# Low parts of weights on GpSimd instead of VectorE, and split products instead of float32 ones, in two sparse-attention layers

## The chip, the core and the metric

The kernel runs on one core of one Trainium2 chip. The metric is the device time of one execution in microseconds. The engines are named as in the profile: PE is TensorE's matmuls, PEld its weight loads, DVE is VectorE, ACT is ScalarE, POOL is GpSimd and SP is SyncE, which issues nearly all transfers.

## The reference

256 tokens of 1024 features go through two models in a row. The first is an mLSTM mixer, a convolutional feed-forward net (FFN), causal attention and a second FFN. The second model is a stack of two equal sparse-attention layers with weights of their own, and the change concerns these two alone. One of them is, in short:

```python
p = h @ w_in[l]                       # h: normalised, modulated input
u_val, u_gate, g_conv, c_q, c_kv, k_idx, w_idx, g_attn = jnp.split(p, offsets, axis=-1)
y_conv = conformer_conv(u_val, u_gate, ...) * silu(g_conv)
                                      # GLU, causal depthwise conv of 31 taps, layer norm, swish, w_pw2
y_attn = dsa_attention(c_q, c_kv, k_idx, w_idx, ...) * silu(g_attn)
                                      # scores of 8 index heads, top 64 keys per query, softmax, values
y = jnp.concatenate([y_conv, y_attn], axis=-1) @ w_out[l]
x = x + gate * rmsnorm(y, g_post[l])
```

All of it is float32, and the output has to agree to float32 accuracy.

## The kernel before, in words

**Products.** A product of two float32 operands is made in one of two ways. A *split* product writes each operand as the sum of a high part, rounded to the shorter format `float32r`, and a low part, the rest. Three matmuls are accumulated: high by high, high by low, low by high (`mm3`, lines 569 to 571). A *float32* product is one matmul instruction on the operands as they are (`mm`, line 422), which shows as two records in the trace.

**Weight pieces.** `Chunk` loads weights from HBM in pieces of up to 128 x 1024 (912 columns for `w_lat`) into a page of pool F. If it is to be split, `split_w` has ScalarE round the piece into one R page (`act`, line 435), and VectorE subtract that from the piece into a second R page (`tt`, line 448). There are 25 F pages and 24 R pages; a piece holds its buffers from the first use to the last.

**A layer.** `dsa_layer` runs once per layer. Its pieces are, in the order of the program: `w_lat` (4 pieces; queries, latent keys and values, index keys), `w_qidx` (1; index queries), `w_u` (4 chunks `u0` to `u3` of 2; gated linear unit), `w_uq` (2; queries), `w_ga` and `w_gc` (2 chunks of 2 each; gates), `w_out` rows 4 to 7 (`oa`, 4; the attention's part of the output projection), `w_pw2` (`pw`, 2; pointwise product of the convolution branch) and `w_out` rows 0 to 3 (`oc`, 4). That makes 33 pieces. The chunks named in `NATIVE`, which are `oa`, `u3`, `w_ga1` and `w_gc1` (10 pieces), are used unsplit in float32 products; the other 23 are split. The attention's four results per layer, which meet `oa`, stay unsplit for the same reason.

**Convolution.** From the four blocks `us` VectorE makes 4 x 30 fused multiply-adds (`stt`, line 453), the taps, with a mean over channels added on the way; the mean goes out to HBM (`zscr`) and back. Then come a sum of squares on PE (operand `con`), the layer norm, `pw` and `oc`.

**Order.** `Program.order` plans at build time. It goes through time with an estimated duration of each instruction, and at each step an engine takes the ready instruction that stands first in the program, if buffers for its results are free. The plan fixes each engine's order; at run time each engine works in that order and waits on semaphores. The taps have late places in the program (`CONV0`, `CONV1`), so they fill VectorE's free time, and top-k has early ones (`TOPK`).

Of the kernel before, what the change touches and what calls it, by code (L numbers as in the profile page):

```python
# [14 lines left out]
ALU = mybir.AluOpType  # L15
# [4 lines left out]
NFF = FF // 128  # L20
# [26 lines left out]
# pages of on-chip memory: name -> (columns, dtype, count)  # L47
# [6 lines left out]
# buffers: name -> (page, part of a page, columns)  # L54
# [33 lines left out]
NATIVE = {"oa", "u3", "w_ga1", "w_gc1"}  # L88
# [4 lines left out]
class Buf:  # L93
    """A slot of a pool from its first to its last use, or a tile of its own (ap given)."""
# [10 lines left out]
class V:  # L105
    """A view of a Buf: rows p0..p1, columns c0..c1, then a function of the access pattern.
    iv: the intervals of columns that it touches, where these are not all of c0..c1."""
# [33 lines left out]
class Program:  # L141
    """Records the kernel's instructions in order, then fixes the order in which each engine issues its own:
    the first in the program among those whose operands and buffers are ready."""
# [39 lines left out]
    @staticmethod  # L183
    def spread(ops, p0, p1):
        """Gives ops the priorities of the program's positions p0..p1."""
        for i, op in enumerate(ops):
            op.prio = p0 + (p1 - p0) * (i + 0.5) / len(ops)

    def order(self, slots):
        """slots: page name -> list of tiles. Returns the ops in the planned order, with table loads."""  # L190
# [30 lines left out]
        # the place for a buffer: an opened page with the least room if it is a small one, else a whole page  # L221
# [160 lines left out]
def build(ctx, tc, a):  # L382
# [57 lines left out]
    # has the activation table ready for what comes after x  # L440
# [70 lines left out]
    # the part of FIRST that begins at each of n columns, then of the next  # L511
# [7 lines left out]
    hold = [None]  # L519

    def split_w(raw, n):
        hi, lo = new("w", n), new("w", n)
        op = act(hi, raw, AF.Copy)
        if hold[0]:
            pg.after(op, hold[0])
        tt(lo, raw, hi.f32, ALU.subtract)
        return hi, lo

    class Chunk:
        """k blocks k0..k1 of a chunk of weights; split, or as it is (native) for a float32 product; cuts: in pieces."""  # L530

        def __init__(self, dram, kc, mc, k0=0, native=False, cuts=None):
            self.mc, self.kp, self.k0 = mc, 1024 // mc, k0
            self.parts = []
            for k in range(k0, kc, self.kp):
# [11 lines left out]
                self.parts.append((raw, None) if native else split_w(raw, n))  # L547
# [12 lines left out]
    # a product of split operands: high*high + high*low + low*high  # L560
# [14 lines left out]
    # two heads' values v[s][e] by their transposed probabilities p[e], each on a half of the partitions (and of the array's columns)  # L575
# [8 lines left out]
    # tokens t of x (stationary) by weights w, token-major  # L584
# [35 lines left out]
    # 1 / sqrt(ms) for a few columns, with a Newton step  # L620
# [10 lines left out]
    # sums over partitions of the squares; n blocks are added before  # L631
# [31 lines left out]
    # products of zeros while the first operands arrive, for the tensor engine's clock  # L663
# [5 lines left out]
    # ================= mLSTM mixer =================  # L669
    # The norm's factor r of a token is left out of the products here: q and the value of h do not depend on it,  # L670
    # k carries it in the exponent, v, o and the gates take it afterwards.
# [11 lines left out]
    # values of the first head, and the gates  # L683
# [134 lines left out]
    # h += w^T x  # L818
# [9 lines left out]
    # ================= conv FFN =================  # L828
# [16 lines left out]
    # quarter q of the token-major copy of h  # L845
# [7 lines left out]
    def ffn(l, h, hm=None, prep=None, head=None):  # L853
# [7 lines left out]
        # the first products start before the norm's factor is known  # L861
        def up(j):
            ps = gemm_pair(Chunk(a["f_w_up"][l * NFF + j], 8, 256), xg if j < HEAD else xs)
# [17 lines left out]
        def down(j):  # L881
            if j == 0:
                acc.extend(psum() for _ in range(4))
            ch = Chunk(a["f_w_down"][l * NFF + j], 1, 1024)
# [37 lines left out]
    # ================= shared keys/values and causal attention =================  # L922
# [19 lines left out]
    # heads' normed and rotated rows (token-major), then transposed  # L942
# [33 lines left out]
    # softmax over keys of -(neg + addm): normalised probabilities, transposed, [s, 256 | 128]  # L976
# [45 lines left out]
    # ================= second block =================  # L1022
    # sums of the four columns 4t..4t+3 into column 4t
# [5 lines left out]
    # 1 / sqrt(mean + EPS) from the parts of a sum of squares, the last of them added on the way  # L1029
# [26 lines left out]
    # the second block's part that needs only one half t of the tokens: norm (token-major), then features on partitions  # L1056
    class Head:
# [8 lines left out]
        # shift and scale of the features; the output's gain as a row  # L1066
# [46 lines left out]
    def prep():  # L1113
        ts(cwh[:, 0:248], cwh[:, 0:248], 0.5, None, ALU.mult)
        # the convolution's bias less its mean over channels
        bsum, bp = small(8), psum()
        mm(bp[:, 0:8], ones, pcols("conv_b_2", 0, 8), True, True)
        vcopy(bsum, bp[:, 0:8])
        for l in range(2):
            sums4(bsum, l)  # L1120
            ts(bcen[:, l * 4:l * 4 + 4], pcols("conv_b_2", l * 4, 4), bsum_scaled(bsum, l), None, ALU.add)
        for hd in heads:
            hd.prep()
# [3 lines left out]
    # relative position bias, as a Toeplitz band: T5[h][p, j] = -bias(128 + p - j)  # L1127
# [19 lines left out]
    def dsa_layer(l, h, last):  # L1147
        hd, xs = heads[l], heads[l].xs
        lw = Chunk(a["w_lat"][l], 8, 456)
# [3 lines left out]
        for t in range(2):  # L1153
            # latent queries, latent keys/values, index keys and weights
# [26 lines left out]
        # index queries, scores  # L1181
        hold[0] = None
        ch = Chunk(a["w_qidx"][l], 2, 512)
# [19 lines left out]
        # top 64 keys of each query  # L1203
# [13 lines left out]
        # convolution branch: gated linear unit, causal depthwise convolution  # L1217
# [3 lines left out]
        for j in range(4):  # L1221
            ps = gemm_pair(Chunk(a["w_u"][l * 4 + j], 8, 256, 0, f"u{j}" in NATIVE), xs)
# [7 lines left out]
        # its mean over channels: sums for each tap, then over taps, each row moved by its tap  # L1230
        # (a channel group's 31 taps and a row of no use on 32 partitions)
# [23 lines left out]
        # queries  # L1255
        hold[0] = None
        ch = Chunk(a["w_uq"][l], 2, 1024)
# [12 lines left out]
        def gate(i):  # L1270
            nme, j = ("w_ga", "w_gc")[i // 2], i % 2
            ps = gemm_pair(Chunk(a[nme][l * 2 + j], 8, 256, 0, f"{nme}{j}" in NATIVE), xs)
# [7 lines left out]
        # attention over the selected keys  # L1280
# [8 lines left out]
        for hp in range(4):  # L1289
# [16 lines left out]
            mix[4 + hp] = (None, None, t) if "oa" in NATIVE else split_x(t)  # L1306
        hd.load_gain()
        # layer norm over channels, swish, pointwise
# [5 lines left out]
        for j in range(4):  # L1314
# [3 lines left out]
            ln.append((None, None, t2) if "pw" in NATIVE else split_x(t2))  # L1318
        preload("E", t2)
        # output projection, attention's part  # L1320
        acc = [[(c0, c1, psum()[:, 0:c1 - c0]) for c0, c1 in zip(cuts, cuts[1:])] for cuts in OCUTS[l]]
        for k in range(4, 8):
            ch = Chunk(a["w_out_2"][l * 8 + k], 1, 1024, 0, "oa" in NATIVE)
# [3 lines left out]
        ch = Chunk(a["w_pw2"][l], 4, 512, 0, "pw" in NATIVE)  # L1327
        for j in range(2):
# [4 lines left out]
            for b in range(2):  # L1333
                t = blk()
                tt(t, half(ps, b), gates[4 + 2 * j + b], ALU.mult)
                mix[2 * j + b] = (None, None, t) if "oc" in NATIVE else split_x(t)
        chs = [Chunk(a["w_out_2"][l * 8 + k], 1, 1024, 0, "oc" in NATIVE) for k in range(4)]
# [130 lines left out]
```

## Time and profile before

| | us |
|---|---|
| three timed runs | 874.07, 874.16, 875.2 |
| median | 874.16 |
| span of the profiled execution (first to last instruction) | 873.5 |
| TensorE matmul busy | 859.4 (98%) |
| VectorE busy | 731.6 (84%) |
| ScalarE busy | 559.4 (64%) |
| GpSimd busy | 0.2 |

The profiled execution's own time is not given apart from its span; it is one of the same kernel whose runs stand 0.6 to 1.7 us above that span. The sparse-attention layers take about the last third of the span; the FFN ahead of them and they overlap in the trace, because weights are loaded and split ahead of their use. An instruction's row gives start and duration; instructions of one engine overlap a little, so the distance from start to start is what one costs its engine. Matmul ends are modelled.

### The profile page before, as it was taken

Reading aid. Unit: us, or ns where it says so; the run is one execution under the profiler, and the core shown is the slowest. Engines: PE = TensorE matmul, PEld = TensorE weight load, DVE = VectorE, ACT = ScalarE, POOL = GpSimd, SP = SyncE. Lnnn points to the kernel's source line nnn. Section 1 sums busy time; section 2 is a strip of 40 time slices with the busy share of each in tenths; the row PEclk is TensorE's granted clock in tenths of the full one; section 3 lists DMA queues with packets and bytes.
Section 4 is the critical chain, followed back from the end, with each engine's and each line's share of the span. In section 5 each row is a group of like instructions: output and inputs, shape, how many; then the busy total and the mean of one; then the engine's idle time right before and its main releaser. Section 6 shows DMA issues by size and latency. Waiting matters only on the chain.

```text
span 873.5 us, 16714 instructions
## 1 busy us (share of the span) xinstructions
PE 859.4 (98%) x6270; PEld 804.2 (92%) x6270; DVE 731.6 (84%) x1677; ACT 559.4 (64%) x1170; POOL 0.2 (0%) x4
## 2 busy tenths in 40 slices
PE   8999999999999999999999999999999999998997
PEld 8999999999999999999989999998998858997866
DVE  6757899899977699987899986675799898798895
ACT  6846577545555496874776546556953797952883
POOL 0000000000000000000000000000000000000000
PEclk9999999999999999999999999999999999999999
DMA  8987766989865354478369985642340177440101
GB/s 317 408 307 228 257 201 200 322 293 319 295 219 179 111 192 134 138 252 301 121 204 355 349 282 175 192 122 86 123 143 13 27 237 302 134 125 13 58 16 49
DMA packets 50409, 170.33 MB, mean 195 GB/s; under 512 B 5860, under 2 KB 8428, under 8 KB 50328
## 3 DMA queue, kind: packets, MB, share of 16 engines
q1 hardware_dynamic: 50184, 169.26, 56.8%
q8 instruction: 49, 0.80, 0.4%
q14 instruction: 32, 0.26, 0.1%
q10 hardware_dynamic: 144, 0.00, 0.0%
HBM read 167.88 MB, written 1.37 MB: 194 GB/s over the span
## 4 chain that ended last, share of the span: by engine, by line
PE 95%; DMA 2%; ACT 1%; DVE 1%; SPq 0%; issue 0%; DVEq 0%; ACTq 0%
PE ps L569 26%; PE ps L570 26%; PE ps L571 26%; PE ps L422 14%; PE ps L426 2%; DMA F<-zscr 1%; PE ps L580 1%; ACT F L435 1%; DMA F<-in_a_w_v_dram 1%; DVE F L453 0%; DMA zscr<-F 0%; ACT R L435 0%; DVE R L448 0%; SPq L1244 0%; PE ps L1237 0%
## 5 line engine op out<-in xcount | busy, mean ns | idle before, releaser
L569 PE MATMUL ps<-R,R 128*128 128x256 f32 (+3 forms) x1788 | 531.8, 297 | 1.3 <-ACT R L435 1.2
L570 PE MATMUL ps<-R,R 128*128 128x256 f32 (+3 forms) x1788 | 522.8, 292 | 0.5 <-DVE R L448 0.5
L571 PE MATMUL ps<-R,R 128*128 128x256 f32 (+3 forms) x1788 | 522.5, 292 | 0.0
L448 DVE TENSOR_TENSOR R<-F,R 128x1024 fp32r<-128x1024 f32 (+4 forms) x339 | 324.3, 983 | 42.0 <-ACT R L435 31.3
L569 PEld LDWEIGHTS ps<-R,R 128*128 128x128 f32 x1788 | 343.5, 192 | 10.2 <-ACT R L435 2.3
L570 PEld LDWEIGHTS ps<-R,R 128*128 128x128 f32 x1788 | 343.7, 192 | 6.8 <-DVE R L448 1.2
L571 PEld LDWEIGHTS ps<-R,R 128*128 128x128 f32 x1788 | 343.4, 192 | 5.7 <-DVE R L448 0.5
L435 ACT ACTIVATE R<-F 128x1024 fp32r<-128x1024 f32 (+4 forms) x339 | 283.1, 864 | 30.6 <-DVE F L448 24.0
L422 PE MATMUL ps<-F,F 128*128 128x256 f32 (+6 forms) x568 | 128.9, 378 | 0.9 <-ACT F L435 0.8
L435 ACT ACTIVATE F<-ps 128x256 f32<-128x256 f32 (+3 forms) x197 | 70.6, 389 | 78.3 <-PE ps L571 37.7
L422 PEld LDWEIGHTS ps<-F,F 128*128 128x128 f32 (+2 forms) x568 | 89.9, 190 | 19.6 <-issue 8.9
L435 ACT ACTIVATE F<-ps,par 128x256 f32<-128x256 f32 (+1 forms) x84 | 42.3, 552 | 93.7 <-PE ps L571 93.3
L453 DVE SCALAR_TENSOR_TENSOR F<-ps,par,F 128x255 f32<-128x255 f32 (+1 forms) x160 | 66.0, 475 | 30.7 <-ACT F L435 30.7
L453 DVE SCALAR_TENSOR_TENSOR F<-F,par,F 128x256 f32<-128x256 f32 (+11 forms) x146 | 66.5, 463 | 1.2 <-ACT F L435 1.2
L435 ACT ACTIVATE F<-F 128x256 f32<-128x256 f32 (+2 forms) x120 | 46.7, 413 | 29.7 <-DVE F L453 17.8
L453 DVE SCALAR_TENSOR_TENSOR F<-F,F 128x1024 f32<-128x1024 f32 x48 | 58.0, 1217 | 0.0
L453 DVE SCALAR_TENSOR_TENSOR F<-F,par 128x255 f32<-128x255 f32 (+14 forms) x126 | 57.8, 460 | 0.0
L448 DVE TENSOR_TENSOR F<-ps,F 128x256 f32<-128x256 f32 (+2 forms) x80 | 32.8, 439 | 21.6 <-PE ps L571 16.2
L435 ACT ACTIVATE F<-F,s 128x128 f32<-128x128 f32 (+1 forms) x80 | 33.3, 445 | 4.9 <-DVE s L474 3.8
L435 ACT ACTIVATE R<-F,par 128x256 fp32r<-128x256 f32 x32 | 14.3, 505 | 28.9 <-DVE F L448 28.9
L1364 ACT ACT_TABLE_LOAD x23 | 29.5, 1283 | 0.4
L426 PE MATMUL ps<-con,F 128*128 128x128 f32 (+2 forms) x158 | 29.4, 271 | 0.1
(96 smaller groups left out, 370.9 us busy)
## 6 DMA issues: line engine op xcount, KB each, us to landing
F<-in_f_w_up_dram SPq DMA_DIRECT2D x88, 512.0 KB, 5.3
F<-in_w_ada_dram SPq DMA_DIRECT2D x48, 512.0 KB, 5.1
F<-in_f_w_down_dram SPq DMA_DIRECT2D x44, 512.0 KB, 5.9
F<-in_w_u_dram SPq DMA_DIRECT2D x16, 512.0 KB, 5.3
F<-in_w_out_dram SPq DMA_DIRECT2D x16, 512.0 KB, 3.8
F<-in_a_w_o_dram SPq DMA_DIRECT2D x8, 512.0 KB, 10.2
F<-in_a_w_out_dram SPq DMA_DIRECT2D x8, 512.0 KB, 10.2
F<-in_w_k_dram SPq DMA_DIRECT2D x8, 512.0 KB, 5.3
```

Source lines behind the costliest of these rows:

```text
L422: pg.add("PE", dur, lambda: nc.tensor.matmul(g(out), g(lhsT), g(rhs), start=start, stop=stop, skip_group_check=not check), [lhsT, rhs], [out])
L426: pg.add("PE", 110.0, lambda: nc.tensor.transpose(g(out), g(x), g(idn)), [x, idn], [out])
L435: nc.scalar.activation(g(out), g(x), func, bias=g(bias), scale=g(scale), **kw)
L448: return pg.add("DVE", ddur(n or x.n), lambda: nc.vector.tensor_tensor(g(out), g(x), g(y), op), [x, y], [out])
L453: nc.vector.scalar_tensor_tensor(g(out), g(x), g(s), g(y), op0, op1, **kw)
L569: nc.tensor.matmul(o, g(lh), g(rh), start=start, stop=False, **kw)
L570: nc.tensor.matmul(o, g(lh), g(rl), start=False, stop=False, **kw)
L571: nc.tensor.matmul(o, g(ll), g(rh), start=False, stop=stop, **kw)
L580: nc.tensor.matmul(g(out[e * 64:e * 64 + 64, c]), g(v[s][e]), g(p[e][:, r]), start=s == 0, stop=s == 1, skip_group_check=True)
L1364: nc.scalar.preload_act_table_set(TABLE[op[1]])
```

## The change

It leaves the first model as it is. In both sparse-attention layers the low part of every weight piece is made by GpSimd instead of VectorE, and the four groups that were float32 products are split like the others, with the results that meet them. The planner books 30 + 2.4 n ns for a subtraction of n columns on GpSimd. FFN chunks now carry names too, none of which is in `BY_POOL`.

```diff
-NATIVE = {"oa", "u3", "w_ga1", "w_gc1"}
+BY_POOL = {"oa","oc","pw","uq","u0","u1","u2","u3","w_ga0","w_ga1","w_gc0","w_gc1","lat","qi"}
...
-    def split_w(raw, n):
+    def split_w(raw, n, by_pool):
         hi, lo = new("w", n), new("w", n)
         op = act(hi, raw, AF.Copy)
         if hold[0]:
             pg.after(op, hold[0])
-        tt(lo, raw, hi.f32, ALU.subtract)
+        if by_pool:
+            pg.add("POOL", 30 + 2.4 * n, lambda: nc.gpsimd.tensor_tensor(g(lo), g(raw), g(hi.f32), ALU.subtract), [raw, hi], [lo])
+        else:
+            tt(lo, raw, hi.f32, ALU.subtract)
         return hi, lo
...
                 load(raw, dram[:, k * mc:k * mc + n])
-                self.parts.append((raw, None) if native else split_w(raw, n))
+                self.parts.append(split_w(raw, n, name in BY_POOL))
...
-            mix[4 + hp] = (None, None, t) if "oa" in NATIVE else split_x(t)
+            mix[4 + hp] = split_x(t)
```

The calls of `Chunk` in `dsa_layer` pass the name instead of the membership in `NATIVE`; nothing else is changed but comments.

## Rows read from the trace of the kernel before

**Rows 1.** The page's busy times: engine, busy us, share of span, instructions.

```profile
PE 859.4 (98%) x6270; PEld 804.2 (92%) x6270; DVE 731.6 (84%) x1677; ACT 559.4 (64%) x1170; POOL 0.2 (0%) x4
```

**Rows 2.** The table by stretches: length, busy of PE, PEld, DVE, ACT, POOL; clock, DMA.

```profile
612.00:636.00 24.00, 24.00 (x171) 22.70 (x170) 18.87 (x31) 22.57 (x58) 0.00 (x0) 1.00 0.46 144
654.00:712.00 58.00, 56.58 (x346) 45.65 (x344) 54.38 (x175) 35.24 (x89) 0.00 (x0) 1.00 0.19 59
740.00:765.00 25.00, 25.00 (x170) 23.10 (x170) 18.95 (x36) 23.82 (x63) 0.00 (x0) 1.00 0.49 149
783.00:844.00 61.00, 57.95 (x360) 47.51 (x360) 55.12 (x178) 37.05 (x91) 0.00 (x0) 1.00 0.09 31
```

**Rows 3.** The same table for line 453 (fused multiply-adds) alone, the tap stretches.

```profile
654.00:712.00 58.00, 48.75 (x125) 1.00 0.19 59
783.00:844.00 61.00, 48.91 (x125) 1.00 0.09 31
```

**Rows 4.** The timeline of layer 1: start, duration, engine, line; VectorE, ScalarE, then TensorE.

```profile
843.23 0.45 DVE L453 SCALAR_TENSOR_TENSOR F<-F,par,F 128x226 f32<-128x226 f32 x1
...
848.68 0.42 ACT L435 ACTIVATE R<-F 128x256 fp32r<-128x256 f32 x1
...
850.58 0.47 PE L569 MATMUL ps<-R,R 128*128 128x256 f32 x1
```

**Rows 5.** The chain of waits, layer 0: start, duration, records of float32 products.

```profile
692.13 0.43 PE ps L422 x2
...
703.80 0.86 PE ps L422 x2
```

**Rows 6.** TensorE's timeline, first matmuls of neighbouring split products, 512 then 256 columns.

```profile
550.91 0.39 PE L569 MATMUL ps<-R,R 128*128 128x512 f32 x1
...
551.59 0.39 PE L569 MATMUL ps<-R,R 128*128 128x512 f32 x1
...
552.98 0.28 PE L569 MATMUL ps<-R,R 128*128 128x256 f32 x1
...
553.34 0.28 PE L569 MATMUL ps<-R,R 128*128 128x256 f32 x1
```

**Rows 7.** Groups by shape, 540 us to the end: count, busy us, mean ns.

```profile
L448 DVE TENSOR_TENSOR R<-F,R 128x1024 fp32r<-128x1024 f32 x55 | 66.2, 1220 | 7.6 <-ACT R L435 4.0 <-issue 3.2 <-PE ps L571 0.3
...
L435 ACT ACTIVATE R<-F 128x1024 fp32r<-128x1024 f32 x54 | 56.3, 1052 | 0.0
...
L448 DVE TENSOR_TENSOR R<-F,R 128x256 fp32r<-128x256 f32 x40 | 16.4, 422 | 11.1 <-ACT R L435 11.1
```

**Rows 8.** VectorE's timeline, subtractions of weight pieces ahead of the tap stretches, both layers.

```profile
634.67 1.23 DVE L448 TENSOR_TENSOR R<-F,R 128x1024 fp32r<-128x1024 f32 x1 [0.27 <-ACT R L435]
...
637.18 1.23 DVE L448 TENSOR_TENSOR R<-F,R 128x1024 fp32r<-128x1024 f32 x1
...
652.29 1.21 DVE L448 TENSOR_TENSOR R<-F,R 128x1024 fp32r<-128x1024 f32 x1
...
764.14 1.23 DVE L448 TENSOR_TENSOR R<-F,R 128x1024 fp32r<-128x1024 f32 x1 [0.33 <-ACT R L435]
...
766.70 1.23 DVE L448 TENSOR_TENSOR R<-F,R 128x1024 fp32r<-128x1024 f32 x1
...
781.82 1.20 DVE L448 TENSOR_TENSOR R<-F,R 128x1024 fp32r<-128x1024 f32 x1
```

**Rows 9.** VectorE's waits in 783 to 844 us: total, times, longest.

```profile
DVE F L464 <- PE ps L422: 2.6, 2, 2.4
DVE F L453 <- PE ps L422: 2.0, 1, 2.0
```

More of the change, by code (lines that the diff above doesn't have):

```diff
@@ L525, in split_w, with __init__ @@
             pg.after(op, hold[0])
-        tt(lo, raw, hi.f32, ALU.subtract)
+        if by_pool:
+            pg.add("POOL", 30 + 2.4 * n, lambda: nc.gpsimd.tensor_tensor(g(lo), g(raw), g(hi.f32), ALU.subtract), [raw, hi], [lo])
+        else:
+            tt(lo, raw, hi.f32, ALU.subtract)
         return hi, lo
     class Chunk:
-        def __init__(self, dram, kc, mc, k0=0, native=False, cuts=None):
+        def __init__(self, dram, kc, mc, k0=0, name=None, cuts=None):
             self.mc, self.kp, self.k0 = mc, 1024 // mc, k0
@@ L862, in up @@
         def up(j):
-            ps = gemm_pair(Chunk(a["f_w_up"][l * NFF + j], 8, 256), xg if j < HEAD else xs)
+            ps = gemm_pair(Chunk(a["f_w_up"][l * NFF + j], 8, 256, 0, f"up{l}{j}"), xg if j < HEAD else xs)
             if j == 0:
@@ L883, in down @@
                 acc.extend(psum() for _ in range(4))
-            ch = Chunk(a["f_w_down"][l * NFF + j], 1, 1024)
+            ch = Chunk(a["f_w_down"][l * NFF + j], 1, 1024, 0, f"down{l}{j}")
             if hm:
@@ L1148, in dsa_layer @@
         hd, xs = heads[l], heads[l].xs
-        lw = Chunk(a["w_lat"][l], 8, 456)
+        lw = Chunk(a["w_lat"][l], 8, 456, 0, "lat")
         lat = [psum() for _ in range(2)]
@@ L1182, in dsa_layer @@
         hold[0] = None
-        ch = Chunk(a["w_qidx"][l], 2, 512)
+        ch = Chunk(a["w_qidx"][l], 2, 512, 0, "qi")
         qix = []
@@ L1221, in dsa_layer @@
         for j in range(4):
-            ps = gemm_pair(Chunk(a["w_u"][l * 4 + j], 8, 256, 0, f"u{j}" in NATIVE), xs)
+            ps = gemm_pair(Chunk(a["w_u"][l * 4 + j], 8, 256, 0, f"u{j}"), xs)
             th, u2, y = blk(), blk(), blk()
@@ L1256, in dsa_layer @@
         hold[0] = None
-        ch = Chunk(a["w_uq"][l], 2, 1024)
+        ch = Chunk(a["w_uq"][l], 2, 1024, 0, "uq")
         qs = []
@@ L1271, in gate @@
             nme, j = ("w_ga", "w_gc")[i // 2], i % 2
-            ps = gemm_pair(Chunk(a[nme][l * 2 + j], 8, 256, 0, f"{nme}{j}" in NATIVE), xs)
+            ps = gemm_pair(Chunk(a[nme][l * 2 + j], 8, 256, 0, f"{nme}{j}"), xs)
             for b in range(2):
@@ L1317, in dsa_layer @@
             act(t2, t, AF.Silu, bias=pcols("conv_ln_b_2", l * 4 + j), scale=pcols("conv_ln_g_2", l * 4 + j))
-            ln.append((None, None, t2) if "pw" in NATIVE else split_x(t2))
+            ln.append(split_x(t2))
         preload("E", t2)
@@ L1322, in dsa_layer @@
         for k in range(4, 8):
-            ch = Chunk(a["w_out_2"][l * 8 + k], 1, 1024, 0, "oa" in NATIVE)
+            ch = Chunk(a["w_out_2"][l * 8 + k], 1, 1024, 0, "oa")
             for t in range(2):
@@ L1326, in dsa_layer @@
                     mm_tm(y, mix[k], ch.at(0, c0, c1), t, k == 4, False)
-        ch = Chunk(a["w_pw2"][l], 4, 512, 0, "pw" in NATIVE)
+        ch = Chunk(a["w_pw2"][l], 4, 512, 0, "pw")
         for j in range(2):
@@ L1335, in dsa_layer @@
                 tt(t, half(ps, b), gates[4 + 2 * j + b], ALU.mult)
-                mix[2 * j + b] = (None, None, t) if "oc" in NATIVE else split_x(t)
-        chs = [Chunk(a["w_out_2"][l * 8 + k], 1, 1024, 0, "oc" in NATIVE) for k in range(4)]
+                mix[2 * j + b] = split_x(t)
+        chs = [Chunk(a["w_out_2"][l * 8 + k], 1, 1024, 0, "oc") for k in range(4)]
         for t in range(2):
```

## The prediction

> **What bounds the kernel now.** I read the page's busy times first: TensorE's matmuls are busy for 859.4 of 873.5 us and GpSimd for 0.2 us [rows 1]. That alone would make this a TensorE kernel, in which every saved product is saved time. The table by stretches says where that is too simple [rows 2]. In 612 to 636 and 740 to 765 us (the start of each layer) PE is busy throughout and VectorE is not. In 654 to 712 and 783 to 844 us (the middle of each layer) VectorE is busy for 54.4 of 58 and 55.1 of 61 us. I call these the tap stretches: 48.8 and 48.9 us of them are fused multiply-adds of one line, 125 of them, nearly all of them the 31-tap convolution [rows 3]. So in the middle of a layer VectorE is as full as PE, and what follows waits for both: the sum of squares over the convolution's result, the layer norm, the product with `w_pw2` and the convolution's part of the output projection. In layer 1 the last tap starts at 843.23 us, the first normalised block is rounded by ScalarE at 848.68, and PE, which fills the gap with the float32 products of `oa`, begins `w_pw2` at 850.58 [rows 4]. That copy and the block's low part on VectorE take 0.42 each [rows 4, 7], so PE could start near 849.6. So the order of things leaves PE about 0.9 us behind the tap chain, no more.
>
> **The change, part by part.**
>
> *Products.* A float32 product of 256 columns is two matmul records, together 0.43 us; one of 512 is 0.86 [rows 5]. A split product of 256 columns recurs every 0.36 us and one of 512 every 0.68 [rows 6]. Per layer `u3`, `w_ga1` and `w_gc1` are 16 products of 256 each, `oa` is 16 of 512 (4 blocks, 2 token halves, 2 pieces): 48 x 0.07 + 16 x 0.18 = 6.3 us per layer off PE, 12.5 in all. All of it lies ahead of `w_pw2`, that is, ahead of the place where PE meets the tap chain.
>
> *Low parts leave VectorE.* Of 33 weight pieces in a layer, 23 were split there at 1.22 us for 1024 columns [rows 7]. Most ran where VectorE has room or PE is the limit, and give nothing. On the chain are those that stand between the scores and the last tap: three per layer, 634.67, 637.18, 652.29 and 764.14, 766.70, 781.82 us [rows 8]. From start to next start each takes 1.15: 3.5 us per layer.
>
> *VectorE's waits.* In the tap stretch of layer 1 it waits 2.6 us for the first logits and 2.0 us for the convolution's mean, both from PE [rows 9]. PE comes to these earlier by 16 x 0.07 = 1.2 us for `u3`, and again for `w_ga1`; a DMA round trip lies ahead of the mean. I count 1.2 us per layer.
>
> *What VectorE and ScalarE get.* Four attention blocks per layer are now split too: a copy on ScalarE and 4 x 0.34 = 1.4 us on VectorE (0.42 each, some 0.08 of it under the next) [rows 7]. Ten more pieces per layer are rounded by ScalarE, 10 x 1.05 = 10.5 us [rows 7]. In the tap stretches it is busy 35.2 of 58 and 37.1 of 61 us, so that is covered; in 612 to 636 and 740 to 765 it is 94 and 95% busy [rows 2], and two rounded pieces too early there would cost 2 us of the score chain. I take 0 and keep the 2 for the range. SP's queue carries the same transfers; a float32 piece kept its F page until its products were done, a split one gives it back after the subtraction but takes two of the 24 R pages instead, so loads move and their bytes do not.
>
> *GpSimd's own time.* No row shows a subtraction on it. The nearest row is VectorE's 1.22 us; the new code's planner books 30 + 2.4 x 1024 = 2488 ns, a plan and no measurement. PE needs 8 x 0.36 = 2.9 or 4 x 0.68 = 2.7 us for the products of one piece, and some eight pieces fit ahead of it in the R pages (24, less four for the features and some four for queries, masks and split results, two per piece). So up to about 2.7 us per piece GpSimd keeps up and its time is hidden; what queues behind it is only PE's second matmul of a product. I price it at nothing, with that cover.
>
> *What GpSimd takes from VectorE.* This decides. No row has both engines on SBUF at once, and GpSimd's subtraction reads two SBUF operands, as each tap on VectorE does. The loss of a tap stretch is bounded below by 0 (work on another engine cannot shorten a tap) and above by the whole of every low part that falls into it. How many: from `w_uq` to `oc` there are 20 pieces per layer, eight of them ready when the taps begin, some three made after them: I count 9. VectorE made its own last one just ahead of each stretch, at 652.29 and 781.82 [rows 8]. At the plan's 2.49 us, and with taps 84% of the stretch (48.8 of 58), the upper end is 9 x 2.49 x 0.84 = 18.8 us per layer. I take one VectorE subtraction's time, 1.22 us per low part, the nearest row: 9 x 1.22 = 11.0 us.
>
> The Trainium skill ("SBUF — State Buffer", section "Who interferes with whom") says that a VectorE instruction with two SBUF inputs and a GpSimd instruction that reads SBUF exclude each other, the later one waiting for the whole of the other. It speaks against this change; no run here shows it, and by it the sum would lie at the upper end. The skill's "GPSIMD Engine Reference" (section 3.1) gives 4497 ns for a two-input add of 2048 columns, so an estimate of 2.25 us for 1024, and the upper end would be 17.0 instead of 18.8.
>
> *Sum.* Relief of VectorE per layer: 3.5 + 1.2 - 1.4 = 3.3 us. Tap chain: +11.0 - 3.3 = +7.7, of which 0.9 goes into the slack: +6.8 per layer, +13.6 for two (layer 0 ends its taps in the same way). PE's 6.3 us per layer become waiting. 873.5 + 13.6 = 887.1 us of span. The median of the runs, 874.16, stands 0.7 above the span: **887.8 us**.
>
> **The rivals.**
>
> *A, the forecast: GpSimd holds VectorE up.* 0.52. For it: two engines that read the same kind of operands in the fullest VectorE stretch. Against: nothing measured. It decides from 4.2 / 1.22 = 3.4 low parts per layer (or 9 at 0.47 us each) upwards. Its own range runs from the break-even, 874, to the upper end: 18.8 - 3.3 - 0.9 = 14.6 per layer, 873.5 + 29.2 + 0.7 = 903.
>
> *B, the other side: no interference.* 0.35. Then the tap chain comes 3.3 us earlier per layer, PE's 6.3 cover that, and the kernel takes 874.2 - 6.6 = 867.6; if the planner moves taps forward as well, all of PE's saving counts: 874.2 - 12.5 = 861.7. For it: the relief stands in rows, and GpSimd has nothing else to do.
>
> *C: GpSimd itself is too slow.* 0.06. The same low part recurs 129.5 us later in the second layer (634.67 and 764.14, [rows 8]), so a layer has 129.5 / 33 = 3.9 us per piece. If a low part takes 4.5 us, 33 need 148.5, and each layer ends 19 us later: 874.2 + 38 = 912. Against it: that is nearly four times VectorE's time.
>
> *D: it cancels.* 0.07. PE's saving becomes waiting and hold-ups near 4.2 us per layer eat the relief: 872.5 to 876.
>
> **How the numbers follow.** About 0.2% (1.7 us) is what a measurement of this kernel can tell from no change. Slower: A and C, 0.58. Faster: B, 0.35. Same: D, 0.07. The range for 8 in 10 takes in both signs: from the bottom of B, 862, to the top of A, 903 (the 2 us of ScalarE lie inside); left out are C and some of the tails. The likeliest case's own range is 874 to 903.
>
> **What would show it.** Step by step: PE's busy time falls by some 12 us if its records stay as they are, and 128x1024 subtractions, 66 of them (8 of 912 columns), stand on POOL. If A holds, the taps, 0.45 us now [rows 4], stretch or start later wherever a POOL row lies over them, VectorE's tap stretch grows from 58 and 61 us towards 66, and PE shows idle time ahead of the sum of squares or `w_pw2`. If B holds, taps keep that duration, the stretches shrink, and the last tap comes some 7 us earlier in the second layer. If C holds, PE waits on POOL. The prediction is wrong if taps under a POOL subtraction keep their time, or if few of POOL's rows fall into the tap stretches.

## The result, and the profile after

The changed kernel takes **939.93 us** (median of 4 runs, 939.23 to 940.48) where the kernel before takes 874.12 in the same comparison: 1.0752 times as long, 95% interval 1.0736 to 1.0768. The forecast was 887.8 us, its range 862 to 903. The sign was right, the size was not: the loss is 65.8 us, not 13.6.

First the page's part 1 (busy times) and two rows of its part 2 (40 slices of the span; GpSimd's busy tenths and TensorE's granted clock).

```profile
PE 865.3 (92%) x6402; PEld 816.8 (87%) x6402; DVE 760.1 (81%) x1639; ACT 578.5 (62%) x1196; POOL 166.5 (18%) x70
...
POOL 0000000000000000000000000268553435657240
PEclk9999999999999999999999999999799797979899
```

Against [rows 1], GpSimd has gone from 0.2 to 166.5 us. VectorE has 38 instructions fewer and is busy 28.5 us longer, although its 46 subtractions of weight pieces have left it and only eight short ones came: its other instructions must have become longer. PE, 98% busy before, is at 92%, and its granted clock, 1.00 in all four stretches of [rows 2], drops again and again in the last third, where GpSimd works.

The table by stretches, first whole, then for line 453 alone, answers to [rows 2, 3]. Its columns are the same; POOL stands fifth and is no longer empty. Only the stretches have other bounds: the tap stretches now run from 663 to 746 and from 830 to 909 us.

```profile
612.00:636.00 24.00, 20.37 (x146) 18.90 (x146) 8.65 (x14) 19.72 (x53) 17.05 (x8) 1.00 0.33 96
663.00:746.00 83.00, 59.35 (x381) 51.18 (x382) 79.03 (x179) 45.59 (x103) 38.58 (x14) 0.87 0.26 84
830.00:909.00 79.00, 57.05 (x382) 49.46 (x382) 74.07 (x177) 42.48 (x99) 35.03 (x14) 0.89 0.01 4
```

```profile
663.00:746.00 83.00, 71.91 (x125) 0.87 0.26 84
830.00:909.00 79.00, 66.11 (x126) 0.89 0.01 4
```

The tap stretches have grown from 58 and 61 to 83 and 79 us, with **14 low parts of GpSimd in each**, and the same 125 fused multiply-adds take 71.9 and 66.1 us instead of 48.8 and 48.9. VectorE is still full: it is longer busy with the same work. PE now idles for over a quarter of these stretches. The groups by shape (540 us to the end; count, busy us, mean ns) say which instructions grew.

```profile
L527 POOL TENSOR_TENSOR R<-F,R 128x1024 fp32r<-128x1024 f32 x58 | 148.8, 2591 | 126.6 <-ACT R L435 52.2 <-issue 36.7 <-PE ps L574 17.3
...
L448 DVE TENSOR_TENSOR R<-F,R 128x256 fp32r<-128x256 f32 x48 | 29.9, 632 | 21.5 <-ACT R L435 21.5
L448 DVE TENSOR_TENSOR F<-ps,F 128x256 f32<-128x256 f32 x32 | 12.6, 419 | 8.0 <-PE ps L574 4.0 <-PE ps L583 2.0 <-ACT F L435 1.7
L453 DVE SCALAR_TENSOR_TENSOR F<-F,par 128x238 f32<-128x238 f32 x6 | 11.1, 1870 | 0.0
```

VectorE's 128x256 subtraction went from a mean of 422 ns [rows 7] to 632, a tap of 238 columns from 459 to 1870. The operation of the same size that reads one operand from PSUM (`F<-ps,F`) stands at 419 ns. That is the pattern everywhere. Over the whole trace 44 of VectorE's instructions are more than 0.15 us longer than the median of their kind before (operation, operands, shape), 77.1 us together; two expectations further down put this sum at 69.9 us, which is too low. GpSimd is at work beside each of the 44, and none of them reads PSUM. All but three, of `TENSOR_SCALAR`, take two operands from SBUF, the on-chip memory that holds pools F and R ("on-chip operand" below means this memory). The timeline shows 21 taps in a row that keep their time, 21 taps in a row of which some do not, then a row of six GpSimd subtractions.

```profile
670.45 8.12 DVE L453 SCALAR_TENSOR_TENSOR F<-F,par 128x250 f32<-128x250 f32 x21
...
682.08 18.16 DVE L453 SCALAR_TENSOR_TENSOR F<-F,par 128x239 f32<-128x239 f32 x21
```

```profile
675.65 18.37 POOL L527 TENSOR_TENSOR R<-F,R 128x1024 fp32r<-128x1024 f32 x6 [9.90 <-PE ps L574]
```

The same number of taps takes 8.1 and 18.2 us. The first subtraction of the six begins beside the first 21 taps and takes 5.97 us: the taps go on undisturbed, and it ends only after VectorE has paused for 2.0 us ahead of 681.41. The other five, 2.4 to 2.6 us each, lie over the first five of the second 21 taps, which take 2.2 to 2.6 us; the sixteen after them take 0.45 again. That is 10.0 us for five subtractions. Not only taps are hit. Ahead of the search for the top 64 keys the index scores are added up on VectorE. Two such additions took 0.7 us together before; now:

```profile
641.40 5.02 DVE L453 SCALAR_TENSOR_TENSOR F<-F,s,F 128x256 f32<-128x256 f32 x2
646.35 2.88 DVE L453 SCALAR_TENSOR_TENSOR F<-F,s 128x256 f32<-128x256 f32 x2
```

Of the 16 additions in layer 0 the first five are longer, by 10.0 us together.

PE's waits from 612 us on (total, times, longest) name VectorE and ScalarE, which waits for VectorE in the softmax; no wait on GpSimd stands in the list.

```profile
PE ps L426 <- ACT F L435: 22.3, 6, 8.8
PE ps L1240 <- DVE F L453: 19.9, 4, 6.6
PE ps L426 <- DVE F L459: 6.6, 1, 6.6
```

The wait at line 1240 is ahead of the convolution's mean, for the gated units. GpSimd does hold up transfers: SyncE waits 86.5 us for its subtractions before it loads into their buffers, where it waited 50.7 us for VectorE's before; but ScalarE's list of waits from 612 us on names no load. VectorE waits for GpSimd once, 5.4 us ahead of the first addition; with fills in GpSimd's place (below) it waits 5.3 us there, for ScalarE.

Where the time went, from five places of VectorE's timeline (us; "search" is the first maximum of a layer's search). The last four rows are runs told of below.

| kernel | search, layer 0 | last tap, layer 0 | search, layer 1 | last tap, layer 1 | end |
|---|---|---|---|---|---|
| before | 642.3 | 712.0 | 771.8 | 843.7 | 873.5 |
| after | 652.5 | 745.6 | 818.7 | 909.4 | 938.2 |
| all split, VectorE alone | 640.4 | 720.7 | 786.7 | 865.5 | 902.3 |
| 46 low parts on GpSimd | 651.6 | 725.5 | 801.0 | 872.9 | 905.7 |
| 20 low parts on GpSimd | 641.2 | 725.7 | 787.9 | 872.4 | 904.0 |
| fills in place of subtractions | 640.2 | 713.7 | 771.5 | 841.9 | 870.6 |

From before to after the five parts grow by 10.2, 23.4, 13.3, 18.8 and -1.1 us, 64.6 in all. 42.2 lie between search and last tap, 23.5 ahead of the searches.

### The profile page after: what moved, and what is told of

The parts are those of the page before. It is cut to its first block, busy times and chain, and to the rows that moved or that the text cites. A ratio compares the mean times of both kernels' runs of the same rounds, so it can differ in the third digit from the quotient of the medians.

```text
span 938.2 us, 17174 instructions
## 1 busy us (share of the span) xinstructions
PE 865.3 (92%) x6402; PEld 816.8 (87%) x6402; DVE 760.1 (81%) x1639; ACT 578.5 (62%) x1196; POOL 166.5 (18%) x70
## 5 line engine op out<-in xcount | busy, mean ns | idle before, releaser
L572 PE MATMUL ps<-R,R 128*128 128x256 f32 (+3 forms) x1920 | 576.9, 300 | 4.2 <-DVE F L448 2.9
L574 PE MATMUL ps<-R,R 128*128 128x256 f32 (+3 forms) x1920 | 565.7, 295 | 4.4 <-DVE R L448 4.4
L573 PE MATMUL ps<-R,R 128*128 128x256 f32 (+3 forms) x1920 | 566.4, 295 | 0.7 <-DVE R L448 0.7
L572 PEld LDWEIGHTS ps<-R,R 128*128 128x128 f32 x1920 | 371.7, 194 | 16.0 <-DVE F L448 3.3
L574 PEld LDWEIGHTS ps<-R,R 128*128 128x128 f32 x1920 | 370.4, 193 | 13.6 <-DVE R L448 7.0
L573 PEld LDWEIGHTS ps<-R,R 128*128 128x128 f32 x1920 | 371.2, 193 | 9.3 <-DVE R L448 2.6
L435 ACT ACTIVATE R<-F 128x1024 fp32r<-128x1024 f32 (+3 forms) x367 | 307.1, 865 | 35.6 <-DVE F L448 28.3
L448 DVE TENSOR_TENSOR R<-F,R 128x1024 fp32r<-128x1024 f32 (+3 forms) x301 | 284.6, 969 | 46.2 <-ACT R L435 35.5
L527 POOL TENSOR_TENSOR R<-F,R 128x1024 fp32r<-128x1024 f32 (+1 forms) x66 | 166.3, 2546 | 744.9 <-ACT R L435 656.7
L453 DVE SCALAR_TENSOR_TENSOR F<-F,par 128x252 f32<-128x252 f32 (+24 forms) x186 | 111.3, 639 | 0.0
L453 DVE SCALAR_TENSOR_TENSOR F<-ps,par,F 128x255 f32<-128x255 f32 (+1 forms) x160 | 66.1, 475 | 32.2 <-ACT F L435 32.2
L426 PE MATMUL ps<-con,F 128*128 128x128 f32 (+2 forms) x158 | 31.0, 283 | 29.0 <-ACT F L435 22.3
L422 PE MATMUL ps<-F,F 128*128 128x128 f32 (+6 forms) x304 | 54.6, 342 | 2.5 <-DVE F L459 2.5
L448 DVE TENSOR_TENSOR F<-ps,F 128x256 f32<-128x256 f32 (+2 forms) x80 | 32.7, 439 | 24.2 <-PE ps L574 18.1
L426 PEld LDWEIGHTS ps<-con,F 128*128 128x128 f32 (+2 forms) x158 | 19.6, 143 | 33.8 <-ACT F L435 24.5
L422 PEld LDWEIGHTS ps<-F,F 128*128 128x128 f32 (+2 forms) x304 | 42.3, 197 | 7.6 <-DVE F L459 2.9
L453 DVE SCALAR_TENSOR_TENSOR F<-F,par,F 128x256 f32<-128x256 f32 (+16 forms) x86 | 45.4, 541 | 1.2 <-ACT F L435 1.2
## 6 DMA issues: line engine op xcount, KB each, us to landing
F<-in_a_w_out_dram SPq DMA_DIRECT2D x8, 512.0 KB, 10.2
```

The costliest lines, as they stand in the source:

```text
L422: pg.add("PE", dur, lambda: nc.tensor.matmul(g(out), g(lhsT), g(rhs), start=start, stop=stop, skip_group_check=not check), [lhsT, rhs], [out])
L426: pg.add("PE", 110.0, lambda: nc.tensor.transpose(g(out), g(x), g(idn)), [x, idn], [out])
L435: nc.scalar.activation(g(out), g(x), func, bias=g(bias), scale=g(scale), **kw)
L448: return pg.add("DVE", ddur(n or x.n), lambda: nc.vector.tensor_tensor(g(out), g(x), g(y), op), [x, y], [out])
L453: nc.vector.scalar_tensor_tensor(g(out), g(x), g(s), g(y), op0, op1, **kw)
L527: pg.add("POOL", 30 + 2.4 * n, lambda: nc.gpsimd.tensor_tensor(g(lo), g(raw), g(hi.f32), ALU.subtract), [raw, hi], [lo])
```

## The experiments

Two theories at first. **Theory 1**: a GpSimd subtraction and a VectorE instruction with two on-chip operands exclude each other (while one runs, the other waits), and this is the whole loss. **Theory 2**: the split products, with the order planned around them, are the loss, whoever makes the low parts. Theory 3 (GpSimd too late for PE) went along.

### The two halves of the change

*All groups split, every low part on VectorE:*

```diff
+NATIVE, BY_POOL = set(), set()
```

> The change without GpSimd: the four float32 weight groups become split products, all 66 low parts are made by VectorE. Theory 1 (GpSimd's subtractions hold VectorE's two-operand instructions up; they are the whole loss): VectorE has ten more low parts per layer at 1.15 us and four split blocks (1.4 us), PE 6.3 us less per layer; if about half of VectorE's new work lies on the tap chain this is some +6 us per layer, 874 to 888 us, and no tap is longer than 0.45 us. Theory 2 (the split products with their new order and their need of pages are the loss, whoever makes the low parts): 925 to 940 us, tap stretches near 80 us.

Measured: 904.84 us, ratio 1.0346 (1.0329 to 1.0364), between the two expectations: 30 us are lost without GpSimd, more than theory 1 left for the products, and less than half of what theory 2 needs. VectorE's timeline at the end of layer 0's taps, then PE's:

```profile
719.84 0.81 DVE L454 SCALAR_TENSOR_TENSOR F<-F,par,F 128x226 f32<-128x226 f32 x2
720.56 3.49 DVE L449 TENSOR_TENSOR R<-F,R 128x1024 fp32r<-128x1024 f32 x3
```

```profile
714.96 1.09 PE L427 MATMUL ps<-con,F 128*128 128x128 f32 x3 [5.83 <-ACT F L436]
715.98 2.19 PE L584 MATMUL ps<-F,F 128*64 128x256 f32 x8
720.85 2.08 PE L423 MATMUL ps<-F,con 128*128 128x256 f32 x4 [2.68 <-ACT F L436]
722.36 0.99 PE L573 MATMUL ps<-R,R 128*128 128x512 f32 x1
```

Taps keep their time (the sum of 120 taps is 55.7 us in layer 0, 55.1 before). But the low parts of `oa` are made behind the last tap, so its products start at 722.36. In the kernel before, `oa` ran in float32 beside the last taps, from 701.8 us. And five low parts stand between search and first tap where one stood, 16.9 us instead of 11.4. So the float32 groups are the ones whose low part has no room on VectorE.

*The float32 groups stay; GpSimd makes the low parts of the other 46 pieces:*

```diff
 NATIVE = {"oa", "u3", "w_ga1", "w_gc1"}
+BY_POOL = {"oc", "pw", "uq", "u0", "u1", "u2", "w_ga0", "w_gc0", "lat", "qi"}
```

> The change without the split products: the float32 groups stay float32, GpSimd makes the low parts of the 46 pieces that were split before. Theory 1: the loss goes by the number of low parts beside taps: 65.8 x 46 / 66 = 46, so 905 to 925 us, and taps and other VectorE instructions with two on-chip operands that lie under a subtraction take up to 2.6 us. Theory 2 (the split products are the loss): 870 to 876 us. Theory 3 (low parts are made too late for PE): as many us lost as theory 1, but in waits of PE for GpSimd, with taps near 0.45 us.

Measured: 908.91 us, ratio 1.0389 (1.037 to 1.0409): within theory 1's bounds, far from theory 2's. VectorE's instructions are 45.9 us longer together. Only five and four low parts lie in the tap stretches. Most of the loss stands ahead of the searches (table: +9.3, and +15.7 between layer 0's last tap and layer 1's search). There short instructions form a chain in which each is waited for. Two rows of VectorE there, and GpSimd's row over the first:

```profile
729.69 3.58 DVE L449 TENSOR_TENSOR F<-F,F 128x256 f32<-128x256 f32 x2 [3.75 <-ACT F L436]
...
762.32 3.77 DVE L454 SCALAR_TENSOR_TENSOR F<-F,s,F 128x256 f32<-128x256 f32 x4
```

```profile
728.38 6.86 POOL L528 TENSOR_TENSOR R<-F,R 128x1024 fp32r<-128x1024 f32 x3 [11.05 <-PE ps L427]
```

*All groups split; GpSimd makes the low parts of the 20 pieces that were float32, VectorE the others:*

```diff
+NATIVE, BY_POOL = set(), {"oa", "u3", "w_ga1", "w_gc1"}
```

> All groups split; GpSimd makes the low parts of the 20 pieces that were float32, VectorE those of the other 46. The changed kernel has 14 low parts beside the taps of each layer, the run with 46 on GpSimd had 4.5, so these ten per layer are those that fall beside the taps. Theory 1: the difference between those two runs, 939.9 - 908.9 = 31 us, comes with these 20 alone: 900 to 910 us, about ten GpSimd rows in each tap stretch, stretches of 73 to 78 us. If it is the split products as such (theory 2): also near 905, but with tap stretches near 62 us and few rows of GpSimd in them.

Measured: 905.62 us, ratio 1.0346 (1.0331 to 1.0362). The time is theory 1's; the count was too high: six rows per tap stretch, not ten, and stretches of 70 us, not 73 to 78. The two runs with GpSimd add up: 20 low parts cost about 30 us, the other 46 about 34, all 66 cost 65.8. What a low part costs thus depends on where it falls: 1.5 us each for these 20, their split products included, 0.74 for those 46. The 20 cost the same 30 us when VectorE makes them (904.84 us), so for them alone GpSimd gains nothing and loses nothing. This run also shows the exclusion most clearly. GpSimd's row of six, then VectorE's taps under it:

```profile
659.36 23.74 POOL L528 TENSOR_TENSOR R<-F,R 128x1024 fp32r<-128x1024 f32 x6 [10.76 <-PE ps L575]
```

```profile
667.85 0.46 DVE L454 SCALAR_TENSOR_TENSOR F<-F,par 128x240 f32<-128x240 f32 x1
668.23 0.75 DVE L454 SCALAR_TENSOR_TENSOR F<-ps,F 128x256 f32<-128x256 f32 x2
668.89 1.95 DVE L454 SCALAR_TENSOR_TENSOR F<-F,par,F 128x239 f32<-128x239 f32 x1
670.77 2.61 DVE L454 SCALAR_TENSOR_TENSOR F<-F,par 128x239 f32<-128x239 f32 x1
...
680.82 2.54 DVE L454 SCALAR_TENSOR_TENSOR F<-F,par 128x237 f32<-128x237 f32 x1
683.28 0.45 DVE L454 SCALAR_TENSOR_TENSOR F<-F,par,F 128x236 f32<-128x236 f32 x1
```

The first of the six begins at 659.36 and takes 11.2 us: 23 taps go on at 0.47 us, one behind the other, until at 668.23 VectorE has two instructions that read PSUM. From then on the engines alternate, one tap per low part: six taps in 14.4 us (668.89 to 683.28) instead of 6 x 0.39 = 2.3. **A low part there costs VectorE (14.4 - 2.3) / 6 = 2.0 us.**

### The exclusion by itself

These runs are the kernel before with GpSimd instructions whose result nobody reads, nine per layer on 512 columns (`dout` and `dgate` are tiles of their own, `con` the constants).

```diff
+    def busy_pool(x):
+        pg.add("POOL", 100.0, lambda: nc.gpsimd.tensor_tensor(g(dgate[:, 0:8]), g(x), g(x), ALU.subtract), [x], [dgate])
+        for _ in range(9):
+            pg.add("POOL", 1260.0, lambda: nc.gpsimd.tensor_tensor(g(dout), g(con[:, 0:512]), g(con[:, 0:512]), ALU.subtract), [con], [dout])
```

The first two runs missed their place: nothing tied the nine to the gate, so GpSimd ran all 18 from 17.6 to 51.1 us.

> The kernel before, plus nine GpSimd subtractions of 512 columns per layer whose result nobody reads, released by the last gated unit, so that they run in the tap stretch; no weight's path is touched. Theory 1: in the changed kernel a tap stretch grew by 24.2 and 19.2 us under 38.9 and 35.9 us of GpSimd's work, 0.58 us per us; here GpSimd works 9 x 1.3 = 11.7 us per stretch, so 6 to 10 us per layer, 885 to 893 us, PE's busy time unchanged. Theories 2 and 3: nothing depends on these instructions, 874 us.

> The same nine subtractions per layer with unused result, released by the first maximum of the top 64 search, where VectorE runs maxima and replacements with one on-chip operand. Theory 1 in its narrow form (only a VectorE instruction with two on-chip operands is held up): 874 to 876 us, maxima and replacements keep their duration. Wide form (any VectorE instruction beside GpSimd is held up): about as much as in the tap stretch, 885 to 893 us.

Measured: 880.70 us, 1.0074 (1.0046 to 1.0102), and 881.15 us, 1.0069 (1.0052 to 1.0086). They test neither place, but say something all the same: at the start of the kernel, where other VectorE work runs, the same 18 subtractions cost some 6 us, and 14.0 us of VectorE's instructions are prolongation. With the gate as an operand (`[con, dgate]`) they ran where they were meant to.

> Again the kernel before with nine GpSimd subtractions of 512 columns per layer whose result nobody reads, now each waiting for the last gated unit, so that they do run beside the taps. In the run in which they ran at the start instead, the shortest took 1.04 us. Theory 1 (a GpSimd subtraction and a VectorE instruction with two on-chip operands exclude each other): 9 x 1.04 = 9.4 us per layer at the most, half of it at the least, less the 0.9 us of slack: 4 to 8.5 us per layer, 882 to 892 us; the taps that meet a subtraction take about 1 us longer. No interference: 873 to 876 us.

Measured: 881.99 us, ratio 1.0080 (1.0061 to 1.0098), at the lower edge of the expectation. VectorE's timeline:

```profile
656.44 0.47 DVE L453 SCALAR_TENSOR_TENSOR F<-F,par,F 128x252 f32<-128x252 f32 x1
656.87 1.22 DVE L453 SCALAR_TENSOR_TENSOR F<-F,par 128x252 f32<-128x252 f32 x1
658.01 1.25 DVE L453 SCALAR_TENSOR_TENSOR F<-F,par,F 128x251 f32<-128x251 f32 x1
...
666.23 1.25 DVE L453 SCALAR_TENSOR_TENSOR F<-F,par 128x248 f32<-128x248 f32 x1
667.40 0.47 DVE L453 SCALAR_TENSOR_TENSOR F<-F,par,F 128x247 f32<-128x247 f32 x1
```

Nine taps in a row, one per subtraction, recur every 1.17 us instead of every 0.39: 0.78 us each, 7.0 per layer. The tap stretches grew by only 5.0 and 1.8 us, since VectorE's waits for PE, 2.6 and 2.0 us in layer 1 [rows 9], are down to 0.2 us: they took up the rest. Here GpSimd did not wait long to begin: its first subtraction takes 1.27 us, the others 1.1.

*18 fills (`memset`) per layer in the same place:*

> The same place, but 18 GpSimd fills of 512 columns per layer that read nothing (result unused). Theory 1 in the form that the two engines exclude each other over operands that they read: 873 to 876 us, taps keep 0.45 us. If any GpSimd work with on-chip memory beside the taps costs VectorE time: as the subtractions per us of GpSimd's work.

Measured: 876.37 us, ratio 1.0002 (0.9985 to 1.0019); not one of VectorE's instructions is longer. GpSimd writing beside the taps costs nothing.

*Nine copies (`tensor_copy`), one operand:*

> As the run with nine unused subtractions beside the taps of each layer, but with copies of 512 columns on GpSimd, which read one on-chip operand. If any GpSimd instruction that reads on-chip memory excludes a tap: taps of 0.47 us become as long as the copy, as under the subtractions. If only two operands on both sides do: taps keep their time, 873 to 877 us.

VectorE's timeline under the copies:

```profile
656.54 0.78 DVE L453 SCALAR_TENSOR_TENSOR F<-F,par 128x252 f32<-128x252 f32 x1
657.25 0.82 DVE L453 SCALAR_TENSOR_TENSOR F<-F,par,F 128x251 f32<-128x251 f32 x1
```

Measured: 874.50 us, ratio 0.9999 (0.9984 to 1.0014), but the taps are longer: 0.82 us in place of 0.47. A GpSimd instruction that reads one operand excludes a tap too; it is only shorter. The 3.1 us of prolongation per layer vanish in the waits of VectorE.

*The nine subtractions beside the search:*

> The nine subtractions per layer, result unused, now each waiting for the first maximum of the top 64 search, so that they run beside maxima and replacements (one on-chip operand each). Theory 1 in the narrow form (only VectorE instructions with two on-chip operands are held up): 873 to 877 us, maxima 0.33 us as before. Wide form: up to 9.4 us per layer on the chain of the search, 882 to 892 us.

Measured: 877.76 us, ratio 1.0025 (1.0009 to 1.0040). Maxima and replacements keep their time beside nine subtractions in a row, as do instructions with one operand in PSUM. One instruction per search is longer. Here it is in this run (groups by shape), then in the kernel before (timeline):

```profile
L480 DVE MAX8 s<-F 128x8 f32<-128x256 f32 x8 | 3.4, 422 | 0.0
...
L460 DVE TENSOR_SCALAR R<-F 128x256 fp32r<-128x256 f32 x1 | 0.9, 948 | 0.0
```

```profile
651.89 0.28 DVE L460 TENSOR_SCALAR R<-F 128x256 fp32r<-128x256 f32 x1
```

It has one on-chip operand and no second one, so "two on-chip operands" is not the whole rule. It needs 0.28 us for 256 columns where a maximum of 256 needs 0.42: it gets through its columns faster. The narrow form holds for the search but for this instruction.

### The changed kernel without the exclusion

Both runs keep every instruction of PE, VectorE and ScalarE where it stands in the changed kernel.

```diff
-nc.gpsimd.tensor_tensor(g(lo), g(raw), g(hi.f32), ALU.subtract)
+nc.gpsimd.tensor_copy(g(lo), g(hi.f32))      (first run)
+nc.gpsimd.memset(g(lo.f32), 0.0)             (second run)
```

> The changed kernel with the same order on PE, VectorE and ScalarE; each GpSimd subtraction is replaced by a copy of the high part into the low part's place (one on-chip operand; the low parts are thus not computed). The copy of 512 columns took 0.70 us and a tap beside it 0.36 us longer. Theory 1: the instruction is 1.3 to 1.4 us instead of 2.5 and costs VectorE half or less: 66 x 0.35 to 0.6 us of VectorE's time in place of 69.9 us, 866 to 890 us. Theory 2 (products and order): 900 us or more remain.

Measured: 879.18 us, ratio 1.0054 (1.0034 to 1.0074). The copy of 1024 columns takes 1.41 us in the mean (1.04 in most rows), and VectorE's instructions are 14.6 us longer together, less than the expected 23 to 40.

> The changed kernel with the same order on PE, VectorE and ScalarE; each GpSimd subtraction is replaced by a fill with zeros (no on-chip operand, so it waits neither for the load nor for the high part; the low parts are not computed). Theory 1: nothing is left of VectorE's 69.9 us of prolongation; what the prediction's rival without interference gave, 862 to 868 us. Theory 2 (products and order): 890 us or more, with taps of 0.47 us.

Measured: **868.75 us, ratio 0.9920 (0.9903 to 0.9936)**, faster than the kernel before and just above the expected 862 to 868. The tables of its tap stretches, whole and for line 454 (the same helper, one line further down):

```profile
650.00:714.00 64.00, 60.20 (x419) 52.66 (x419) 56.48 (x181) 45.71 (x103) 15.62 (x17) 0.97 0.32 108
781.00:842.00 61.00, 58.91 (x435) 52.61 (x433) 56.47 (x180) 42.93 (x101) 12.15 (x13) 1.00 0.02 6
```

```profile
650.00:714.00 64.00, 48.96 (x125) 0.97 0.32 108
781.00:842.00 61.00, 49.21 (x126) 1.00 0.02 6
```

17 and 13 instructions of GpSimd lie beside the taps, and the taps take 49 us again. In the whole run only two of VectorE's instructions are longer beside a fill, both `TENSOR_SCALAR` with one on-chip operand of 128 columns: 0.62 and 0.63 us instead of 0.28. Between this run and the changed kernel lie 939.9 - 868.8 = **71.2 us**, and the instruction on GpSimd is the only difference: what it reads, how long it takes and what it waits for. The copy, which waits for the high part as the subtraction does, has 60.8 of these us back. So theory 2 is out as a cause in the changed kernel. The fill could also start earlier than a subtraction could, so a little of the last 10 us may be lateness; how much stays open.

### Two attempts to do better

*The order planned with the exclusion in it* (the planner starts such an instruction of either engine only when the other's has ended):

```diff
+            if op.two:
+                start = max(t, lock)
+                lock = start + op.dur
```

> The changed kernel, but the program that fixes the instructions' order is told that a GpSimd subtraction and a VectorE instruction with two on-chip operands never overlap, so that it orders the work around it. Theory 1 with the exclusion as a fixed price (66 low parts of 2.5 us, and VectorE has no spare time beside the taps): little comes back, 915 to 938 us. If most of the loss comes from an order that was planned for engines that don't disturb each other: 880 to 905 us.

Measured: 962.92 us, ratio 1.1014 (1.0990 to 1.1038): worse than both expectations. VectorE's prolongation is still 72.4 us, and PE waits longer, now 34.7 us for ScalarE in the softmax (22.3 in the changed kernel) and 10.3 us for high parts (0.5). From PE's list of waits, 640 us to the end:

```profile
PE ps L432 <- ACT F L441: 34.7, 9, 12.4
...
PE ps L578 <- ACT R L441: 10.3, 6, 3.8
```

So knowing of the exclusion did not remove its price here. Why the order itself came out worse was not looked into.

*The kernel before with two low parts per layer moved to GpSimd, beside the search* (the planner's rule of the run above is in this run too, so the order beside these two is planned with it):

```diff
+BY_POOL = {"w_gc0.1", "pw.0"}
```

> The kernel before with two low parts per layer moved to GpSimd, those that VectorE makes beside the top 64 search (652.29 us and the one that follows in the plan); the float32 groups stay. In the run with unused subtractions beside the search maxima and replacements kept their time, one short instruction per search lost 0.7 us. Theory 1: VectorE gains 2 x 1.15 us per layer and loses 0 to 0.7: 870.5 to 874 us. If moving any low part costs (wide form): 876 to 880 us.

Measured: 874.19 us, ratio 1.0009 (0.9997 to 1.0021): no difference, and just above what theory 1 gave. No VectorE instruction is longer. Layer 0's first tap comes at 652.47 instead of 653.68, its last ends at 712.2 instead of 712.0. The gain is given back inside the tap stretch, where VectorE waits for PE, by the list of its waits from 652 to 713 us (the same wait was 1.2 us before):

```profile
DVE F L459 <- PE ps L428: 2.2, 1, 2.2
```

*`oa` alone stays float32, no GpSimd:*

```diff
+NATIVE, BY_POOL = {"oa"}, set()
```

> No GpSimd; u3, w_ga1 and w_gc1 are split by VectorE, only oa stays float32. In the run with all groups split by VectorE PE stood still beside the last taps, since the low parts of oa were made only after the last tap. Theory 4 (starvation: oa in float32 is the work that PE can do while VectorE is full): most of the 30 us is back, 876 to 886 us, PE busy beside the last taps. If the loss goes by the number of low parts added to VectorE (12 of 20): 874 + 18 = 892 us.

Measured: 891.38 us, ratio 1.0202 (1.0186 to 1.0218). Theory 4 falls as the main cause: each run against the kernel before beside it, 12 low parts cost 17.6 us and 20 cost 29.9, so `oa` in float32 brings back 12.3 us, its share of the low parts (8 of 20). The loss follows the number of low parts that VectorE has to make.

## Why the prediction was wrong in size

**The mechanism was right.** Forecast A said that GpSimd holds VectorE up, and named what would show it: taps longer than 0.45 us under a GpSimd row, tap stretches growing, PE idle ahead of the sum of squares or `w_pw2`. The first two stand in the trace. The third does in layer 0 alone, 4.3 us ahead of the sum of squares; most of PE's idle time stands ahead of the convolution's mean and inside the softmax, which wait for VectorE without needing the last tap. **The rival without interference** said 867.6 us, and the run without the exclusion took 868.75. Its condition held, but that the figures meet is luck, as its terms did not come out (below). Three steps of the sum failed.

1. *The price of a low part beside taps.* "I take one VectorE subtraction's time, 1.22 us per low part, the nearest row." It is 2.0 us: GpSimd's subtraction takes 2.35 us undisturbed in the shortest rows and 2.59 in the mean, and only one tap of 0.39 slips in behind each. The nearest row was the wrong engine's. The upper end (2.49 us times the taps' share of 84% is 2.1) was near.

2. *The count.* "I count 9." It was 14 in each stretch. With the earlier rate of 1.22 us this alone would have made 17.1 instead of 11.0 us per layer; with 2.0 us it makes 28. From first to last tap the stretches grew by 24.2 and 19.2, since some of the low parts lie over waits and over instructions that read PSUM: 12 and 11 of VectorE's instructions were hit, and became 23.0 and 19.1 us longer. The count alone put the range too low: with 14 low parts its upper end, 18.8 us per layer, would have been 29.3.

3. *Where it was counted at all.* Only the tap stretches were charged: "The loss of a tap stretch is bounded." The other low parts were priced at nothing, as hidden behind PE. But the sum of index scores, the residual and the norm between the layers are chains of short VectorE instructions with two on-chip operands; each one that meets a low part waits for most of it (2.1 us for four of the first five additions of scores). The places ahead of the searches cost 10.2 + 13.3 = 23.5 us of the 64.6, over a third, and these came on top of the stretches, which had already passed the upper end.

The Trainium skill ("SBUF — State Buffer", section "Who interferes with whom") was set beside the sum as the end that no row yet showed: the two instructions exclude each other, and the later one waits for the whole of the other. The runs agree: 0.47 us becomes 2.5 under a subtraction of 1024 columns, 1.25 under one of 512, 0.82 under a copy of 512, and stays 0.47 beside a fill. The same section says that a VectorE instruction with at most one such input, outside its two-port modes, does not contend. The maxima, 422 ns beside subtractions and 415 without, agree. The `TENSOR_SCALAR` instructions that became longer agree if their faster pace is such a mode, which no run here shows. One thing goes beyond a wait for the whole of the other: GpSimd waited for 23 taps in a row, not for one.

The smaller steps. *GpSimd's own time hidden*: held; PE's list of waits has no GpSimd row in it, and rival C is out. *VectorE's relief* of 3.3 us per layer: not borne out as put. In the run without the exclusion VectorE's first tap of layer 0 comes 3.4 us earlier, yet the last one ends at 713.7 instead of 712.0: it waits 4.3 us for PE at the convolution's mean, where it waited 1.2 before. Moving two low parts per layer without any hold-up brought nothing either (874.19 us). The profiled execution of the run with fills, 872.4 us and the longest of its five, ends 2.9 us earlier than the kernel before: by the table 2.1 of them come ahead of layer 0's search and 2.0 between its last tap and layer 1's search, while 3.8 are lost between search and last tap of layer 0. Where the rest of the 6.2 us between the medians comes from is open. *PE's products*: PE's busy time is 853.1 us in that run, 6.3 below [rows 1], about half of the 12.5 reckoned. In the changed kernel it is 865.3, with a granted clock of 0.87 and 0.89 in the tap stretches: parts of them run at 1.2 GHz instead of 2.4, and PE stood idle first. From 690 to 699.8 us, for one, it is busy for 4.6 of 9.8 us at a granted clock of 1.00, and in the 6.9 us that follow the granted clock is 0.51. What that adds beside the exclusion wasn't separated; with the exclusion gone, the clock is back at 0.97 and 1.00.

## What to carry to other kernels

An idle engine is not a free one: before work goes to GpSimd, look at what VectorE runs beside it, and count each GpSimd instruction that reads on-chip memory at its whole duration, less one VectorE instruction, wherever VectorE's instructions take two on-chip operands and something waits for them. Charge this in every stretch in which the moved work falls, not only in the fullest one. The cheapest test is a few GpSimd instructions with an unused result in the stretch in question, or the finished change with a fill in place of the moved operation.

## What was not expected of the hardware

- The engines do not always take turns from the start. With 20 low parts on GpSimd its first subtraction beside the taps stood 11.2 us, 8.9 of them through 23 taps in a row, until VectorE had an instruction with an operand in PSUM; in the changed kernel one stood 5.97 us, until VectorE paused. Once GpSimd had got in, every tap waited for a whole subtraction. The unused subtractions of 512 columns got in at once (1.27 us for the first); what decides this was not tested.
- A subtraction of 1024 columns takes GpSimd 2.35 us in the shortest rows, a copy 1.04 (1.41 in the mean of its run), a fill 0.96.
- A VectorE instruction with a single on-chip operand can be held up too: a `TENSOR_SCALAR` of 256 columns went from 0.28 us to 0.95 beside a subtraction, and one of 128 columns from 0.28 to 0.62 beside a fill, which leaves the taps alone.
